# An encoder trunk on one core: order of the first loads, zero products on TensorE, and the place of the sink values' negation

## The chip, the core and the metric

The kernel runs on one NeuronCore of a Trainium2 chip. The metric is the device time of one execution in microseconds (us). The kernel before took 1389.4 us, the median of three runs (1389.08 to 1389.6).

## What is computed

The program is two layers of an encoder over 512 tokens of width 1024, all in float32:

```
for l in range(2):
    h = rms_norm(x, attn_norm_g[l])
    z = h @ w_in[l]                       # q, k, v of two attentions, two gates
    qa, ka, va, qb, kb, vb, ga, gb = split(z)
    qa, ka = rope(rms_norm(qa)), rope(rms_norm(ka))     # cos/sin of positions
    ya = window_gqa(qa, ka, va, sink_a[l]) @ w_proj_a[l]
    yb = neighbourhood_attn(rms_norm(qb), rms_norm(kb), vb, rel_bias_b[l]) @ w_proj_b[l]
    x = x + (sigmoid(ga) * ya + sigmoid(gb) * yb) @ w_out[l]
    h = rms_norm(x, ffn_norm_g[l])
    x = x + (silu(h @ w_gate[l]) * (h @ w_up[l])) @ w_down[l]
```

The sink is one extra logit per head in the softmax of the first attention; the softmax there needs the sink values and their negation.

## The kernel before

**Number format.** Every float32 product is made of three products in a faster format: each factor is split into a high part (a rounding copy, on ScalarE) and a low part (the difference, on VectorE), and high x high, high x low and low x high are added up in PSUM. So an operand costs a copy on ScalarE and a subtraction on VectorE, and each 128x512 tile of a product costs three matmuls.

**Start of the program.** x comes in eight chunks of 128 columns (`x_load`, SyncE's DMA queue, 256 KB each). The first product is q of layer 0: for each chunk k the routine `start` (line 1174) transposes the four 128x128 blocks of the chunk on TensorE, ScalarE writes the high part of the scaled chunk, the copy xT and its square, and VectorE writes the low part and adds up the squares. Then four groups of three matmuls (one per token block b = 0 to 3) use chunk k. `token_matmul` (line 881) calls `start(k + 1)` behind the group of b = 0, so that in TensorE's queue the transposes of chunk k + 1 stand between the group b = 0 of chunk k and its groups b = 1, 2, 3. The engines take their instructions in the order in which they are written; one that waits holds back all behind it on its engine.

**The first weights.** The four slabs of `w_in` that this product needs (two chunks of rows each) are loaded whole and split on the engines (`first_load`, `first_parts`, lines 529 and 541): slab 0 through ScalarE's queue in two transfers, slabs 1 to 3 through GpSimd's. GpSimd's queue also brings the positions, the head norms' gains, the sinks and the rest of the constants (`cst[:, P:]`, line 735, which has the table of rotary frequencies). The identity for the transposes comes first on SyncE's queue (line 709).

**Norm gains.** `attn_norm_g` and `ffn_norm_g` are loaded as 32 rows of 128 (`vec`, line 711, ScalarE's queue, ahead of slab 0), transposed at once, and read as columns of `vecT` by `gain` (line 742). ScalarE needs the first of them for the high part of chunk 0.

**Tables.** `chain_tables` (line 751) prepares what the heads need: it copies the positions into rows 64 to 67 of `vec2`, negates the sinks (`nsnk`, line 754), transposes `vec2` on TensorE (line 758; the head gains and positions turn into columns, `vec2T`), and works out sine and cosine on VectorE and ScalarE (lines 765 to 782) from `vec2T` and `cst`. It is a generator: a planner with a cost model runs the program once without emitting it, and between two groups of matmuls it lets a chain go on when its `Need` is met, by the model's times of the tiles that it names. The order found is then the program's order on every engine. The model keeps one time per tile, that of its last writer in program order. So `Need("pe", [vec2])` looks at the copy of the positions on VectorE, which is the last to write `vec2`; the hardware waits of the transpose go by all writers of `vec2`, transfers among them.

Of the kernel before, what the change touches and what calls it, by code (L numbers as in the profile page):

```python
# [12 lines left out]
F32 = mybir.dt.float32  # L13
# [3 lines left out]
ALU = mybir.AluOpType  # L17
AX = mybir.AxisListType

P = 128  # L20
# [4 lines left out]
NB = S // P  # L25
# [61 lines left out]
def by_columns(ap):  # L87

    return ap.rearrange("p (r cc c) -> p cc r c", r=8, c=8)


def held(ap):
    return ap.rearrange("p (cc r c) -> p cc r c", r=8, c=8)
# [116 lines left out]
def trunk(ctx: ExitStack, tc: tile.TileContext, a: dict, out: bass.AP, lay: Layout):  # L210
    nc = tc.nc
    PS = bass.MemoryType.PSUM
    cp = ctx.enter_context(tc.tile_pool(name="cp", bufs=1))
# [7 lines left out]
    def nm(s):  # L221
        uid[0] += 1
        return f"{s}_{uid[0]}"
# [7 lines left out]
    def buf(shape, dtype=F32):  # L231

        n = int(np.prod(shape))
        x = lay.place(n, dtype)
        t = arenas[dtype][:, x : x + n]
        if len(shape) == 2:
            t = t.rearrange("p (a b) -> p a b", b=shape[1])
        elif len(shape) == 3:
            t = t.rearrange("p (a b c) -> p a b c", b=shape[1], c=shape[2])
        return t  # L240
# [4 lines left out]
    def act(dtype=F32):  # L245
        return buf([S], dtype)

    def mm_bank():
        return pm.tile([P, S], F32, tag="mm", name=nm("mm"))

    def at_bank():
        return pa.tile([P, S], F32, tag="at", name=nm("at"))
# [42 lines left out]
    def touch(aps, start, end):  # L295
        for x in aps:
            o = name_of(x)
            if isinstance(o, int):
                lay.touch(o, steps[0], start, end)
# [36 lines left out]
    T = Engine(nc.tensor, "pe")  # L336
    V = Engine(nc.vector, "dve")
    A = Engine(nc.scalar, "act")
    G = Engine(nc.gpsimd, "pool")
    Q = Engine(nc.sync, "dma")  # L340
    AQ = Engine(nc.scalar, "dma")
# [187 lines left out]
    def first_load(i):  # L529

        n1, n2, ((_, ap),) = plan[i]
        raws[i] = buf([n1, n2])
        ap = ap.rearrange("(k p) n -> p k n", p=P)
        if i:
            GQ.dma_start(raws[i], ap)
        else:
            for k in range(2):
                AQ.dma_start(raws[i][:, k], ap[:, k])
        highs[i], lows[i] = buf([n1, n2], F32R), buf([n1, n2], F32R)

    def first_parts(k):
        raw, h, lo = raws[k // 2][:, k % 2], highs[k // 2][:, k % 2], lows[k // 2][:, k % 2]
        A.copy(h, raw)
        V.tensor_tensor(lo, raw, h.bitcast(F32), ALU.subtract)
# [142 lines left out]
    ident = cst[:, C_ID : C_ID + P]  # L687
    rev = cst[:, C_REV : C_REV + P]
    rev2 = cst[:, C_REV + 64 : C_REV + 64 + P]
    maskA = cst[:, C_MA : C_MA + 3 * P]  # L690
    vec = cp.tile([32, P], F32, tag="vec", name="vec")
    vec2 = cp.tile([P, P], F32, tag="vec2", name="vec2")
    vecT = cp.tile([P, 32], F32, tag="vecT", name="vecT")
    vec2T = cp.tile([P, P], F32, tag="vec2T", name="vec2T")
    ones = cp.tile([P, 2], F32, tag="ones", name="ones")
    magic = cp.tile([P, 32], I32, tag="magic", name="magic")
    G.memset(vec2, 0.0)
    G.memset(ones, 1.0)
    G.memset(magic, 0x5F3759DF)
# [3 lines left out]
    def x_load(c):  # L703
        t = act().rearrange("p (b n) -> p b n", b=NB)
        Q.dma_start(t, xv[:, :, P * c : P * c + P])
        xin.append(t)


    Q.dma_start(ident, a["consts"][:, :P])
    for i, n in enumerate(("attn_norm_g", "ffn_norm_g")):  # L710
        AQ.dma_start(vec[16 * i : 16 * i + 16], a[n].rearrange("l (k p) -> (l k) p", p=P))
    first_load(0)
    for c in range(KD):
        x_load(c)
    posi = cp.tile([P, P], I32, tag="posi", name="posi")
    for h in range(2):
        GQ.dma_start(
# [12 lines left out]
    gqa = cp.tile([P, 2, DEPTH, HD], F32, tag="gqa", name="gqa")  # L730
    for i, n in enumerate(("q_norm_a", "k_norm_a")):
        GQ.dma_start(gqa[:, i], a[n].rearrange("l d -> (l d)").unsqueeze(0).to_broadcast([P, DEPTH * HD]))
    snk = cp.tile([P, DEPTH, 8], F32, tag="snk", name="snk")
    GQ.dma_start(snk, a["sink_a"].rearrange("l h -> (l h)").unsqueeze(0).to_broadcast([P, DEPTH * 8]))
    GQ.dma_start(cst[:, P:], a["consts"][:, P:])
    warm = cp.tile([P, 2], F32, tag="warm", name="warm")
    A.copy(warm, ones)
    ps = at_bank()
    T.transpose(ps[:, :32], vec, ident[:32, :32])
    V.tensor_copy(vecT, ps[:, :32])  # L740

    def gain(norm, k):
        c = 16 * (norm % 2) + 8 * (norm // 2) + k
        return vecT[:, c : c + 1]

    xT = [buf([S]) for _ in range(KD)]
    nsnk = cp.tile([P, DEPTH, 8], F32, tag="nsnk", name="nsnk")
    gb = cp.tile([P, DEPTH], F32, tag="gb", name="gb")
    trig = cp.tile([P, 2, NB, 32], F32, tag="trig", name="trig")

    def chain_tables():
        yield Need("dve", [posi, snk, gqa])
        V.tensor_copy(vec2[64:68], posi[64:68])
        V.tensor_scalar(nsnk, snk, -1.0, None, ALU.mult)
        yield Need("pe", [vec2], [at_slots])
        at_slots.take()
        ps = at_bank()
        T.transpose(ps[:, :P], vec2, ident)
        yield Need("dve", [ps])
        V.tensor_copy(vec2T, ps[:, :P])  # L760
        at_slots.give(clock["dve"])
        posf = vec2T[:, 64:68]
        V.scalar_tensor_tensor(gb, vec2T[:, 0:2], HD ** -0.5, vec2T[:, 2:4], ALU.mult, ALU.mult)
        v3 = lambda t: t[:, : NB * 32].rearrange("p (b f) -> p b f", b=NB)
        ang = v3(act())
        for b in range(NB):
            V.tensor_scalar(ang[:, b, :], cst[:, C_INV : C_INV + 32], posf[:, b : b + 1], None, ALU.mult)
        yield Need()
        for i, shift in enumerate((0.25, 0.0)):
            n, r = v3(act()), v3(act())  # L770
            V.tensor_scalar(n, ang, INV_2PI, shift, ALU.mult, ALU.add)
            V.tensor_scalar(n, n, ROUND_MAGIC, None, ALU.add)
            V.tensor_scalar(n, n, -ROUND_MAGIC, None, ALU.add)
            yield Need()
            V.scalar_tensor_tensor(r, n, -TWO_PI_1, ang, ALU.mult, ALU.add)
            V.scalar_tensor_tensor(r, n, -TWO_PI_2, r, ALU.mult, ALU.add)
            V.scalar_tensor_tensor(r, n, -TWO_PI_3, r, ALU.mult, ALU.add)
            yield Need()
            if shift:
                V.tensor_scalar(r, r, HALF_PI, None, ALU.add)  # L780
            V.tensor_scalar(r, r, PI_LO, -PI_LO, ALU.min, ALU.max)
            A.activation(trig[:, i], r, AF.Sin)
            yield Need()
        done.add("trig")


# [31 lines left out]
    class Norm:  # L818
# [8 lines left out]
        def chunk(self, k):  # L827
            split(xT[k], self.xh[k], self.xl[k], scale=gain(self.i, k))
            sq = act()
            A.activation(sq, xT[k], AF.Square)  # L830
            if self.acc is not None:
                V.tensor_tensor(sq, sq, self.acc, ALU.add)
            self.acc = sq
            if k == KD - 1:
                done.add(f"acc{self.i}")
# [338 lines left out]
    def start(nrm, k):  # L1174

        ps = at_bank()
        for b in range(NB):
            T.transpose(ps[:, P * b : P * b + P], xin[k][:, b, :], ident)
        if k:
            first_parts(k)  # L1180
        A.activation(held(nrm.xh[k]), by_columns(ps), AF.Copy, scale=gain(0, k))
        if not k:
            first_parts(k)
        A.copy(held(xT[k]), by_columns(ps))
        V.scalar_tensor_tensor(nrm.xl[k], xT[k], gain(0, k), nrm.xh[k].bitcast(F32), ALU.mult, ALU.subtract)
        sq = act()
        A.activation(sq, xT[k], AF.Square)
        if nrm.acc is not None:
            V.tensor_tensor(sq, sq, nrm.acc, ALU.add)
        nrm.acc = sq  # L1190
        if k == KD - 1:
            done.add("acc0")

    def layer(l):
# [158 lines left out]
        if l == 0:  # L1353
            spawn(chain_tables())
# [366 lines left out]
```

## Time and profile before

| what | us |
|---|---|
| median of 3 runs | 1389.4 (1389.08 to 1389.6) |
| the profiled execution, its own time | 1389.13 |
| its span, first to last instruction | 1387.4 |
| TensorE busy, share of the span | 1370.7, 99% |
| VectorE busy | 910.7, 66% |
| ScalarE busy | 708.3, 51% |
| first matmul of a product | 6.80 after the start |

The profiled execution's own time is 1.7 us above its span: that is what lies before the first and behind the last instruction. TensorE (PE in the rows) is the engine that sets the time nearly everywhere; what it misses at the start it doesn't make up. In rows of the timeline the first number is the start, the second the duration in us; "out<-in" are the tiles, buffer numbers left out, so `vec` stands for `vec` and `vec2` alike; x4 is a count; brackets hold the idle time of the engine ahead of the row and who ended it. A duration of several merged rows reaches to the end of the last.

### The profile page before, as it was taken

How to read it: one execution, taken by the hardware profiler on the slowest of the kernel's cores; microseconds unless marked ns; L12 is line 12 of the kernel's file. 1: busy time of each engine (PE TensorE's matmuls, PEld its weight loads, DVE VectorE, ACT ScalarE, POOL GpSimd, SP SyncE). 2: the span in 40 equal slices, each digit the busy share in tenths (PEclk: the TensorE clock that was granted, in tenths of full speed). 3: DMA queues.
4: the chain of work that ended last, by engine and by line, in shares of the span. 5: the costliest groups of instructions: out<-in, count | busy, mean ns of one | idle time of the engine just before them, and what ended most of it. 6: DMA issues, size and time to landing. Idle time of an engine off the chain costs nothing.

```text
span 1387.4 us, 20895 instructions
## 1 busy us (share of the span) xinstructions
PE 1370.7 (99%) x8042; PEld 1211.2 (87%) x8042; DVE 910.7 (66%) x1702; ACT 708.3 (51%) x1171; POOL 317.3 (23%) x326
## 2 busy tenths in 40 slices
PE   8999999999999999999999999999999999999998
PEld 6888888888899999999888888888888999999996
DVE  5875878555976657575648667784578757575663
ACT  6476667634643333343545675675356434333441
POOL 4542222310221110111353422223012110111110
PEclk9999999999999999999999999999999999999999
DMA  8998888864766484735899978879457583654645
GB/s 213 183 172 142 158 161 155 173 165 127 151 148 152 106 197 93 182 93 106 160 189 188 166 140 160 155 140 217 142 121 151 123 213 88 156 122 121 146 86 119
DMA packets 197331, 207.45 MB, mean 150 GB/s; under 512 B 25568, under 2 KB 167056, under 8 KB 197232
## 3 DMA queue, kind: packets, MB, share of 16 engines
q0 software_dynamic: 134976, 141.54, 54.6%
q1 hardware_dynamic: 61904, 64.04, 15.9%
q8 instruction: 63, 1.03, 0.3%
q10 hardware_dynamic: 352, 0.54, 0.1%
q14 instruction: 36, 0.29, 0.1%
HBM read 193.51 MB, written 2.10 MB: 141 GB/s over the span
## 4 chain that ended last, share of the span: by engine, by line
PE 90%; DVE 2%; issue 2%; ACT 2%; DMA 2%; POOL 0%; POOLq 0%; ACTq 0%
PE mm L310 71%; PE at L310 19%; ACT arena L310 2%; DVE arena L310 2%; DMA arena<-in_w_down 1%; DMA arena<-in_w_in 1%; DVE sm L310 0%; DMA cst<-in_consts 0%; POOL arena L310 0%; ACT L310 0%; POOL posi L310 0%; POOL vec L310 0%; DVE mm L310 0%; ACT trig L310 0%; ACT sm L310 0%
## 5 line engine op out<-in xcount | busy, mean ns | idle before, releaser
L310 PE MATMUL mm<-arena 128*128 128x512 f32 (+1 forms) x5568 | 1113.1, 355 | 5.8 <-DVE mm L310 3.4
L310 PEld LDWEIGHTS mm<-arena 128*128 128x128 f32 x5568 | 905.0, 190 | 140.7 <-DVE arena L310 4.1
L310 ACT CAST arena<-arena 128x1024 fp32r<-128x1024 f32 (+2 forms) x278 | 235.3, 869 | 213.8 <-DVE arena L310 207.7
L310 DVE TENSOR_TENSOR arena<-arena,arena 128x1024 fp32r<-128x1024 f32 (+2 forms) x268 | 262.1, 993 | 52.1 <-ACT arena L310 51.4
L310 PE MATMUL at<-arena 128*128 128x256 f32 (+1 forms) x1952 | 282.8, 289 | 0.4 <-DVE negm L310 0.4
L310 ACT ACTIVATE arena<-arena 128x1024 fp32r<-128x1024 f32 (+3 forms) x252 | 206.7, 843 | 149.4 <-DMA arena<-in_w_down 77.0
L310 PEld LDWEIGHTS at<-arena 128*128 128x128 f32 x1952 | 259.9, 191 | 13.6 <-DVE negm L310 1.4
L310 DVE TENSOR_TENSOR arena<-arena,mm 128x512 f32<-128x512 f32 x144 | 98.9, 686 | 241.8 <-PE mm L310 240.3
L310 POOL DMA_DIRECT2D arena<-in_w_in x163 | 162.2, 1370 | 303.4 <-ACT arena L310 281.7
L310 POOL DMA_DIRECT2D arena<-in_w_down x96 | 98.1, 1224 | 505.4 <-ACT arena L310 376.7
L310 DVE TENSOR_TENSOR arena<-arena 128x1024 f32<-128x1024 f32 (+4 forms) x196 | 158.0, 823 | 2.4
L310 DVE TENSOR_TENSOR arena<-at,arena 128x512 fp32r<-128x512 f32 (+4 forms) x158 | 104.3, 660 | 30.6 <-ACT arena L310 24.1
L310 ACT CAST arena<-at 128x512 fp32r<-128x512 f32 (+2 forms) x116 | 64.4, 555 | 63.7 <-PE at L310 62.4
L310 PE MATMUL at<-cst,arena 128*128 128x128 f32 x472 | 74.0, 276 | 1.8 <-issue 1.4
L310 ACT ACTIVATE arena<-arena,negm 128x256 f32<-128x256 f32 (+1 forms) x128 | 68.2, 534 | 14.4 <-DVE negm L310 12.4
L310 ACT COPY arena<-at 128x512 f32<-128x512 f32 (+1 forms) x68 | 39.5, 581 | 64.5 <-PE at L310 64.0
L310 PEld LDWEIGHTS at<-cst,arena 128*128 128x128 f32 x472 | 58.1, 141 | 11.9 <-issue 1.8
L310 DVE TENSOR_TENSOR arena<-mm,arena 128x512 f32<-128x512 f32 x72 | 49.1, 686 | 25.3 <-PE mm L310 25.1
L310 DVE CUSTOM_DVE_ANT_0 arena<-at,cst,nsnk 128x256 f32<-128x256 f32 (+1 forms) x64 | 34.4, 547 | 35.0 <-PE at L310 34.4
L310 ACT ACTIVATE arena<-arena,vecT 128x512 fp32r<-128x512 f32 x24 | 17.4, 726 | 54.8 <-DVE arena L310 54.4
L310 DVE CUSTOM_DVE_ANT_0 arena<-at,arena 128x256 f32<-128x256 f32 x64 | 26.3, 420 | 17.3 <-PE at L310 17.0
L310 POOL DMA_DIRECT2D arena<-in_w_up x8 | 8.2, 1030 | 126.7 <-PE mm L310 79.1
(68 smaller groups left out, 423.2 us busy)
## 6 DMA issues: line engine op xcount, KB each, us to landing
arena<-in_w_in POOLq DMA_DIRECT2D x99, 512.0 KB, 7.4
arena<-in_w_down POOLq DMA_DIRECT2D x80, 512.0 KB, 6.7
arena<-in_w_gate SPq DMA_DIRECT2D x20, 1024.0 KB
arena<-in_w_up SPq DMA_DIRECT2D x20, 1024.0 KB
arena<-in_w_in POOLq DMA_DIRECT2D x64, 256.0 KB, 6.4
arena<-in_w_proj_a POOLq DMA_DIRECT2D x16, 512.0 KB, 7.3
arena<-in_w_proj_b POOLq DMA_DIRECT2D x16, 512.0 KB, 7.1
arena<-in_w_out SPq DMA_DIRECT2D x16, 512.0 KB
```

The costliest lines, as they stand in the source:

```text
L310: f(*args, **kw)
```

## The change

- `vec` holds only `attn_norm_g`, 16 rows, and comes on SyncE's queue behind the identity and ahead of x. `ffn_norm_g` goes into rows 32 to 47 of `vec2`, on SyncE's queue behind the eight chunks of x; `gain` reads it from `vec2T`.
- The two transfers of slab 0 are the first on ScalarE's queue.
- The high and low part of slab 0's first rows are written ahead of those of x's chunk 0, as the other chunks have it already.
- Seven float32 products of zeros, 128x128, are put ahead of the first transpose, and three behind the transposes of chunk 0. Their operand is the tile `trig`, cleared by GpSimd as its first act and later overwritten by the cosines.
- The negation of the sinks stands behind the sine and cosine; the first `Need` of the chain names the positions alone.

```diff
+    def turn_over(n):
+        ps = mm_bank()
+        for _ in range(n):
+            T.matmul(ps[:, :P], idle, idle, start=True, stop=True)
+
+    G.memset(idle, 0.0)
     G.memset(vec2, 0.0)
...
+    first_load(0)
     Q.dma_start(ident, a["consts"][:, :P])
-    for i, n in enumerate(("attn_norm_g", "ffn_norm_g")):
-        AQ.dma_start(vec[16 * i : 16 * i + 16], a[n].rearrange("l (k p) -> (l k) p", p=P))
-    first_load(0)
+    Q.dma_start(vec, a["attn_norm_g"].rearrange("l (k p) -> (l k) p", p=P))
     for c in range(KD):
         x_load(c)
+    Q.dma_start(vec2[32:48], a["ffn_norm_g"].rearrange("l (k p) -> (l k) p", p=P))
...
     A.copy(warm, ones)
+    turn_over(7)
     ps = at_bank()
-    T.transpose(ps[:, :32], vec, ident[:32, :32])
+    T.transpose(ps[:, :16], vec, ident[:16, :16])
...
     def gain(norm, k):
-        c = 16 * (norm % 2) + 8 * (norm // 2) + k
-        return vecT[:, c : c + 1]
+        t, c = (vec2T, 32) if norm % 2 else (vecT, 0)
+        c += 8 * (norm // 2) + k
+        return t[:, c : c + 1]
...
     def chain_tables():
-        yield Need("dve", [posi, snk, gqa])
+        yield Need("dve", [posi])
         V.tensor_copy(vec2[64:68], posi[64:68])
-        V.tensor_scalar(nsnk, snk, -1.0, None, ALU.mult)
         yield Need("pe", [vec2], [at_slots])
...
             A.activation(trig[:, i], r, AF.Sin)
             yield Need()
+        yield Need("dve", [snk, gqa])
+        V.tensor_scalar(nsnk, snk, -1.0, None, ALU.mult)
         done.add("trig")
...
-        if k:
-            first_parts(k)
+        if not k:
+            turn_over(3)
+        first_parts(k)
         A.activation(held(nrm.xh[k]), by_columns(ps), AF.Copy, scale=gain(0, k))
-        if not k:
-            first_parts(k)
         A.copy(held(xT[k]), by_columns(ps))
```

Behind the first twenty microseconds the instructions of both programs stand in the same order on every engine, apart from `vec2T` in the place of `vecT` where the FFN's gains are read. Three places of the start show what moves.

SyncE's queue, as a difference, first rows of the program: `vec` is the tile of `attn_norm_g`, `vec_76` is `vec2`, `arena_72` takes x.

```order
 L310 DMA cst<-in_consts 128x128
+L310 DMA vec<-in_attn_norm_g 16x128
 L310 DMA arena_72<-in_x 128x4x128 x8
+L310 DMA vec_76<-in_ffn_norm_g 16x128
 L310 DMA arena_73<-arena_73 64x512 x4
```

The two gains now stand on this queue, one ahead of the eight chunks of x, the other behind them.

TensorE before, from the group b = 0 of chunk 1 to the transposes of chunk 3 (`mm_2` to `mm_5` are the banks of the token blocks 0 to 3, `at_8` and `at_10` the transposes of the chunks 2 and 3, `at_9_181` the transpose of `vec2`; DMAHW and DMASW are counters of transfers, HW of the queues of SyncE and ScalarE, SW of GpSimd's):

```order
L310 MATMUL mm_2_121<-arena1_73 128x512 [waits Activation_49]
L310 MATMUL mm_2_121<-arena1_73 128x512 [waits DVE_49] x2
L310 MATMUL at_8_166<-cst_74,arena0_72 128x128 [waits DMAHW7_49]
L310 MATMUL at_8_166<-cst_74,arena0_72 128x128 x3
L310 MATMUL mm_3_122<-arena1_73 128x512 x3
L310 MATMUL at_9_181<-cst_74,vec2_76 128x128 [waits DMASW5_49,DMASW3_49,DMASW6_49,DMASW2_49,DVE_49]
L310 MATMUL mm_4_123<-arena1_73 128x512 x3
L310 MATMUL mm_5_124<-arena1_73 128x512 x3
L310 MATMUL mm_2_121<-arena1_73 128x512 [waits Activation_49]
L310 MATMUL mm_2_121<-arena1_73 128x512 [waits DVE_49] x2
L310 MATMUL at_10_199<-cst_74,arena0_72 128x128 [waits DMAHW0_49,PE_49]
```

The same piece of TensorE's queue now (`mm_3` to `mm_6` are the banks, `at_10` and `at_12` the transposes of the chunks 2 and 3, `at_11_190` the transpose of `vec2`):

```order
L310 MATMUL mm_3_130<-arena1_73 128x512 [waits Activation_49]
L310 MATMUL mm_3_130<-arena1_73 128x512 [waits DVE_49] x2
L310 MATMUL at_10_178<-cst_74,arena0_72 128x128 [waits DMAHW6_49]
L310 MATMUL at_10_178<-cst_74,arena0_72 128x128 x3
L310 MATMUL at_11_190<-cst_74,vec2_76 128x128 [waits DMASW5_49,DMASW6_49,DMASW3_49,DMAHW4_49,DMASW2_49,DVE_49]
L310 MATMUL mm_4_131<-arena1_73 128x512 x3
L310 MATMUL mm_5_132<-arena1_73 128x512 x3
L310 MATMUL mm_6_133<-arena1_73 128x512 x3
L310 MATMUL mm_3_130<-arena1_73 128x512 [waits Activation_49]
L310 MATMUL mm_3_130<-arena1_73 128x512 [waits DVE_49] x2
L310 MATMUL at_12_211<-cst_74,arena0_72 128x128 [waits DMAHW7_49]
```

The transpose of `vec2` has moved up by one group of three matmuls, and among its waits there is a new one on a counter of the hardware queues, DMAHW4: the transfer of `ffn_norm_g`.

VectorE, as a difference, around the copy of the positions (`vec_76` is `vec2`; the three rows behind `nsnk` are the low parts of slab and x and the sum of squares, for chunk 2):

```order
 L310 TENSOR_TENSOR arena_72<-arena_72 128x512
 L310 CAST vec_76<-posi 4x128
-L310 TENSOR_SCALAR nsnk<-snk 128x16
 L310 TENSOR_TENSOR arena_73<-arena_72,arena_73 128x512
 L310 SCALAR_TENSOR_TENSOR arena_73<-arena_72,vecT,arena_73 128x512
```

The negation no longer stands ahead of chunk 2's parts; it comes back behind the second sine.

More of the change, by code (lines that the diff above doesn't have):

```diff
@@ L690, in trunk @@
     maskA = cst[:, C_MA : C_MA + 3 * P]
-    vec = cp.tile([32, P], F32, tag="vec", name="vec")
+    vec = cp.tile([16, P], F32, tag="vec", name="vec")
     vec2 = cp.tile([P, P], F32, tag="vec2", name="vec2")
-    vecT = cp.tile([P, 32], F32, tag="vecT", name="vecT")
+    vecT = cp.tile([P, 16], F32, tag="vecT", name="vecT")
     vec2T = cp.tile([P, P], F32, tag="vec2T", name="vec2T")
@@ L696, in trunk @@
     magic = cp.tile([P, 32], I32, tag="magic", name="magic")
+    trig = cp.tile([P, 2, NB, 32], F32, tag="trig", name="trig")
+    idle = trig[:, 0].rearrange("p b f -> p (b f)")
+    def turn_over(n):
[3 more added lines that the diff above has]
+    G.memset(idle, 0.0)
     G.memset(vec2, 0.0)
@@ L737, in trunk @@
     A.copy(warm, ones)
+    turn_over(7)
     ps = at_bank()
-    T.transpose(ps[:, :32], vec, ident[:32, :32])
-    V.tensor_copy(vecT, ps[:, :32])
+    T.transpose(ps[:, :16], vec, ident[:16, :16])
+    V.tensor_copy(vecT, ps[:, :16])
     def gain(norm, k):
-        c = 16 * (norm % 2) + 8 * (norm // 2) + k
-        return vecT[:, c : c + 1]
+        t, c = (vec2T, 32) if norm % 2 else (vecT, 0)
+        c += 8 * (norm // 2) + k
+        return t[:, c : c + 1]
     xT = [buf([S]) for _ in range(KD)]
@@ L748, in trunk @@
     gb = cp.tile([P, DEPTH], F32, tag="gb", name="gb")
-    trig = cp.tile([P, 2, NB, 32], F32, tag="trig", name="trig")
     def chain_tables():
-        yield Need("dve", [posi, snk, gqa])
+        yield Need("dve", [posi])
         V.tensor_copy(vec2[64:68], posi[64:68])
-        V.tensor_scalar(nsnk, snk, -1.0, None, ALU.mult)
         yield Need("pe", [vec2], [at_slots])
```

## The prediction

> **What bounds the kernel now.** I read the page first, then the chain of waits, then the timelines of the first 40 us, since every changed line acts there. The page's first rows:
>
> ```profile
> span 1387.4 us, 20895 instructions
> PE 1370.7 (99%) x8042; PEld 1211.2 (87%) x8042; DVE 910.7 (66%) x1702; ACT 708.3 (51%) x1171; POOL 317.3 (23%) x326
> ```
>
> PE is busy for all but 16.7 us. So what PE loses or saves at the start should come out at the end one for one. The chain of waits, taken up to 60 us, says from where:
>
> ```profile
> 3.94 7.82 DMA arena<-in_w_in
> 11.75 0.28 issue
> 12.04 4.75 DMA cst<-in_consts
> ...
> 36.16 1.02 PE at L310 x8
> 37.18 4.23 PE mm L310 x18
> ```
>
> Transfers lead up to about 17 us; from 36 us on the chain is PE behind PE. Now PE alone, in order of time ("mm" matmuls of the product, "at" transposes):
>
> ```profile
> 4.09 0.28 PE L310 MATMUL at<-cst,vec 32*128 32x32 f32 x1 [4.09 <-DMA vec<-in_ffn_norm_g]
> 4.40 1.12 PE L310 MATMUL at<-cst,arena 128*128 128x128 f32 x4
> 6.80 2.18 PE L310 MATMUL mm<-arena 128*128 128x512 f32 x3 [1.28 <-ACT arena L310]
> 8.78 1.05 PE L310 MATMUL at<-cst,arena 128*128 128x128 f32 x4
> 9.48 4.53 PE L310 MATMUL mm<-arena 128*128 128x512 f32 x12
> 13.86 0.60 PE L310 MATMUL at<-cst,arena 128*128 128x128 f32 x4
> 14.21 0.94 PE L310 MATMUL mm<-arena 128*128 128x512 f32 x3
> 14.99 0.27 PE L310 MATMUL at<-cst,vec 128*128 128x128 f32 x1
> 15.02 1.85 PE L310 MATMUL mm<-arena 128*128 128x512 f32 x7
> 17.55 0.50 PE L310 MATMUL mm<-arena 128*128 128x512 f32 x1 [0.68 <-DVE arena L310]
> ...
> 18.55 0.60 PE L310 MATMUL at<-cst,arena 128*128 128x128 f32 x4
> 18.90 3.02 PE L310 MATMUL mm<-arena 128*128 128x512 f32 x12
> 21.76 0.60 PE L310 MATMUL at<-cst,arena 128*128 128x128 f32 x4
> ```
>
> Three losses: PE stands until 4.1; it runs slow up to about 13 (four transposes take 1.1 us, later 0.6); and at 17.5 it waits for VectorE. The slow clock by itself, the matmuls from 10.1 to 12.6 us:
>
> ```profile
> 9.48 3.33 PE L310 MATMUL mm<-arena 128*128 128x512 f32 x7
> ```
>
> Seven slow matmuls take 3.33 us, seven fast ones (15.02) 1.85: 0.21 us more for each. VectorE's wait:
>
> ```profile
> 12.45 0.22 DVE L310 CAST vec<-posi 4x128 f32<-4x128 int32 x1
> 16.72 0.17 DVE L310 TENSOR_SCALAR nsnk<-snk 128x16 f32<-128x16 f32 x1 [4.05 <-DMA snk<-in_sink_a]
> 18.68 0.28 DVE L310 COPY vec2T<-at 128x128 f32<-128x128 f32 x1
> 19.07 0.67 DVE L310 TENSOR_SCALAR arena<-cst,vec2T 128x32 f32<-128x32 f32 x4
> 19.66 0.68 DVE L310 TENSOR_TENSOR arena<-arena,arena 128x512 fp32r<-128x512 f32 x1
> ```
>
> The negation of the sinks holds chunk 2's parts back for 4.05 us. The change takes this wait away.
>
> **The change part by part.** First what it puts ahead. SyncE's and ScalarE's queues:
>
> ```profile
> 1.19 0.44 ACTq L310 DMA_DIRECT2D vec<-in_ffn_norm_g  x1
> 1.20 6.67 SPq L310 DMA_DIRECT2D arena<-in_x  x8
> ...
> 1.66 1.09 ACTq L310 DMA_DIRECT2D arena<-in_w_in  x2
> ```
>
> Slab 0 is issued 0.92 us earlier (1.66 to 0.74); x about 0.44 later, the price of one small issue. The ten products of zeros stand where PE is idle: seven before 4.1, where PE waits for the gains, three behind the first transposes, where it waits 1.28 for ScalarE. No row shows one; between a slow transpose (1.12 / 4 = 0.28) and a slow 512-column matmul (0.48) seven take 2.0 to 3.3 us and three 0.8 to 1.4, so at worst 0.1 shows. They should bring the fast clock some microseconds ahead, worth up to 9 x 0.21 = 1.9 us on the nine matmuls of chunk 0 behind 9.48. Putting slab 0's copy ahead takes one copy of some 0.6 us from PE's wait at 6.80. GpSimd's memset delays its transfers by about 0.2 us. The narrower `vec` and the other place of the FFN gains cost nothing: same instructions, 100s of us before their use. All of this brings PE earlier to the transpose of `vec2`: to about 12 us if all of it works, 14.5 if none does (transposes of chunk 2 now end at 13.86 + 0.60).
>
> Now what PE meets there. The transpose of `vec2` is ahead of three groups of chunk 1 (nine matmuls) and waits for `ffn_norm_g`, which is on SyncE's queue behind all of x. When is that queue done? DMA rows of two stretches, 17 to 17.5 us and 17.5 to 18 (q1 is SyncE's queue; the second stretch has no row of it):
>
> ```profile
> q1 hardware_dynamic: 39, 0.02, 13.0%
> ```
>
> ```profile
> q0 software_dynamic: 137, 0.18, 154.0%
> ```
>
> The last bytes of x move at about 17.4, nearly 10 us after the last issue, because GpSimd's slabs share the engines. x's first chunk was there at 4.4 (PE's transposes), with the other seven already issued or on their way: the queue serves in order of issue. So 8 KB behind x land at about 18.0: last bytes 17.4, and some tenths for its own packets and its signal. The bounds: 17.5 (the start of x's traffic is fuller now) and 18.8 (0.44 later issue, packets of GpSimd's queue in between). No row of this case shows two transfers of one queue in conflict. [...]
>
> So PE stands from 12 to 18.0, and all that was won before is spent there. Behind it: the transpose (0.3), then 9 matmuls of chunk 1 and 3 of chunk 2, ready long since, before the transposes of chunk 3. Twelve take 21.76 - 18.90 = 2.86 now. Chunk 3's transposes start at 18.0 + 0.3 + 2.86 = 21.16, in place of 18.55: **+2.6 us**. VectorE's turn: the copy of `vec2T` comes at about 18.4 (18.68 now), so the tables and chunk 3's low part (19.66) stay where they were and are no longer late for PE. `nsnk` itself, 0.17, hides beside PE.
>
> The clock. What a pause does to it shows at the end of the program: PE's last rows, and the column PEclk (the third number from the end) in three stretches:
>
> ```profile
> 1380.44 0.60 PE L310 MATMUL at<-cst,arena 128*128 128x128 f32 x4
> 1382.46 0.63 PE L310 MATMUL at<-cst,arena 128*128 128x128 f32 x4 [1.42 <-issue]
> ```
>
> ```profile
> 1381.00:1384.00 3.00, 0.67 (x5) 0.42 (x4) 1.28 (x2) 0.59 (x1) 0.00 (x0) 1.00 0.51 159
> 1384.00:1385.00 1.00, 0.00 (x0) 0.00 (x0) 0.00 (x0) 0.00 (x0) 0.00 (x0) 0.96 0.29 93
> 1385.00:1386.00 1.00, 0.00 (x0) 0.00 (x0) 0.00 (x0) 0.00 (x0) 0.00 (x0) 0.50 0.53 169
> ```
>
> The clock halves at 1384.9 (0.96 is 0.08 us at half), 3.9 us after the last dense work and in spite of four transposes in between. A pause of 6 us is longer, so I take it that PE resumes slow. How long? At the start it became fast near 12.7, after work without a gap since about 8.2: 4.5 us. At 0.476 us a matmul these are 9.5 matmuls, times 0.21: **+2.0 us**. Bounds: 0, and 3.0 if it takes as long as from the first matmul (6.80) to 12.7. [...]
>
> From chunk 3's transposes on, both programs have the same order and the same dependences (transposes, ScalarE's copies, VectorE's low part, products), and the chain is PE: I give nothing back and add nothing. Sum, on the profiled execution's own 1389.13: +2.6 +2.0 = +4.6, **1393.7**. The median is 0.27 above that execution, within what three runs scatter.
>
> **Rivals.**
> - *The clock stays fast over the pause*, or PE comes so late (14.5) that the pause is under 3.9 us. Then +2.6 alone: 1391.7. For it: the fall was seen once only. Against: 6 is well over 3.9.
> - *The gains come early* and PE doesn't stop. The point that decides is about 15.5 us: landing + 0.3 + 2.86 = 18.55. Its place is next VectorE's table step, which reads `cst`:
>
> ```profile
> cst<-in_consts POOLq DMA_DIRECT2D x1, 336.0 KB, 6.7
> ```
>
> Issued at 12.04, it is there at 18.7. Chunk 3's low part follows at 18.7 + 0.6, against 19.66 now; PE, done with chunk 2 at some 16.5, waits for it, and chunk 3's products end 0.4 to 0.7 earlier than now: 1388.6. So the wait for the sinks was hiding a wait for the constants. For it: only an overtaking on SyncE's queue. Against: x's first chunk landed first.
> - *All the change is for*: gains early, and `cst` 3 us sooner because slab 0 leaves the queues sooner. Then the 0.6 of the copy, 1.9 of the clock and the 1.6 that PE now stands or runs late between 16.9 and 18.5 are won: 4.1, 1385.0. It needs two transfers to land earlier than any row suggests.
>
> **How the numbers follow.** Forecast (pause and slow clock) 0.78, pause alone 0.12, gains early 0.07, all won 0.03. The range reaches from the second case with a landing at 17.6 (1391.3) to a landing at 18.8 with the longest slow time (1389.13 + 3.4 + 3.0 = 1395.5): 1391.3 to 1395.6. A measurement of this kernel tells about 0.2% (2.8 us) from no change, so "slower" begins at 1392.2. Slower: nearly all of the forecast and a fifth of the second case, 0.80. Same: the rest of the second and the third, 0.17. Faster: 0.03.
>
> **What would show it.** In the new profile: no wait of `nsnk`; the first product before 6.8; at the transpose of `vec2` a pause of 5 to 6 us, ended by `in_ffn_norm_g` near 18; the matmuls behind it at 0.43 to 0.48 each for 4 to 5 us; chunk 3's transposes near 23.2 in place of 18.55; the start of the sums (36.16) later by the same 4.6. Wrong if that pause is missing or ends before 15.5, or if PE's distance shrinks between chunk 3 and 41 us.

## The result, and the profile after

The changed kernel takes 1396.17 us (median of six, 1395.32 to 1398.66), the kernel before 1389.41 (median of six, 1389.08 to 1390.05): a ratio of 1.0051, with a 95% interval of 1.0040 to 1.0061. It is slower by 6.8 us where 4.3 on the median (4.6 on the profiled execution) were forecast, and just outside the range. Its profiled execution took 1396.52, the span in it:

```profile
span 1393.3 us, 20937 instructions
PE 1373.8 (99%) x8062; PEld 1215.1 (87%) x8062; DVE 911.2 (65%) x1702; ACT 708.0 (51%) x1171; POOL 317.5 (23%) x327
```

So the span grew by 5.9 us; the rest of that execution's 7.4 lies outside it (3.2 us now, 1.7 before). TensorE in order of time, the rows that answer to those of before:

```profile
5.68 1.11 PE L310 MATMUL at<-cst,arena 128*128 128x128 f32 x4 [1.11 <-DMA arena<-in_x]
7.73 1.74 PE L310 MATMUL mm<-arena 128*128 128x512 f32 x3
9.31 0.60 PE L310 MATMUL at<-cst,arena 128*128 128x128 f32 x4
9.66 3.01 PE L310 MATMUL mm<-arena 128*128 128x512 f32 x12
12.52 0.60 PE L310 MATMUL at<-cst,arena 128*128 128x128 f32 x4
19.63 0.45 PE L310 MATMUL at<-cst,vec 128*128 128x128 f32 x1 [6.51 <-DMA vec<-in_ffn_norm_g]
19.73 4.44 PE L310 MATMUL mm<-arena 128*128 128x512 f32 x12
24.00 0.60 PE L310 MATMUL at<-cst,arena 128*128 128x128 f32 x4
```

The pause is there, at the transpose of `vec2`, and the FFN's gains end it, at 19.63. The chain of waits runs through the same transfer, from its issue to its landing:

```profile
7.49 12.01 DMA vec<-in_ffn_norm_g
19.50 0.14 issue
19.63 0.45 PE at L310
20.08 4.09 PE mm L310 x12
...
41.61 1.02 PE at L310 x8
```

The clock around the pause (stretches of 1 us; the third number from the end is the granted clock, 1.00 or 0.50, so a mean of 0.60 is 0.8 us at half):

```profile
15.00:16.00 1.00, 0.00 (x0) 0.00 (x0) 0.70 (x2) 0.49 (x1) 0.00 (x0) 0.99 1.08 323
16.00:17.00 1.00, 0.00 (x0) 0.00 (x0) 0.00 (x0) 0.00 (x0) 0.00 (x0) 0.50 1.20 370
22.00:23.00 1.00, 1.00 (x4) 0.81 (x3) 0.00 (x0) 0.00 (x0) 0.00 (x0) 0.60 0.00 0
```

It halves at 15.98 and is back at 22.80, 3.2 us behind the end of the pause. VectorE no longer waits for the sinks:

```profile
37.97 0.17 DVE L310 TENSOR_SCALAR nsnk<-snk 128x16 f32<-128x16 f32 x1
```

The transposes of chunk 3 start 5.45 us later than before (24.00 against 18.55), and the ones-sums too (41.61 against 36.16). By the end 0.45 us more have come on, about half of it at a pause near 390 us (1.89 us long, 1.66 in before).

### The profile page after: what moved, and what is told of

Its sections match the earlier page's. It is cut to its first block, busy times and chain, and to the rows that moved or that the text cites. A ratio compares the mean times of both kernels' runs of the same rounds, so it can differ in the third digit from the quotient of the medians.

```text
span 1393.3 us, 20937 instructions
## 1 busy us (share of the span) xinstructions
PE 1373.8 (99%) x8062; PEld 1215.1 (87%) x8062; DVE 911.2 (65%) x1702; ACT 708.0 (51%) x1171; POOL 317.5 (23%) x327
## 4 chain that ended last, share of the span: by engine, by line
PE 90%; DVE 2%; ACT 2%; issue 2%; DMA 2%; SPq 0%; POOL 0%; DVEq 0%; POOLq 0%; ACTq 0%
PE mm L310 71%; PE at L310 19%; ACT arena L310 2%; DVE arena L310 2%; DMA arena<-in_w_down 1%; DMA vec<-in_ffn_norm_g 1%; SPq L310 0%; DVE sm L310 0%; POOL arena L310 0%; ACT L310 0%; DVE mm L310 0%; ACT trig L310 0%; DVEq L1728 0%; ACT sm L310 0%; DVE den L310 0%
## 5 line engine op out<-in xcount | busy, mean ns | idle before, releaser
L310 ACT ACTIVATE arena<-arena,vec2T 128x512 fp32r<-128x512 f32 x16 | 11.6, 726 | 47.5 <-DVE arena L310 47.5
```

The costliest lines, as they stand in the source:

```text
L310: f(*args, **kw)
```

## The experiments

Thirteen kernels, each beside runs of the kernel before on the same chip. "Ratio" is to before, with its 95% interval; "span" is that of the profiled execution.

| kernel | edit, in words | median, us | ratio | span |
|---|---|---|---|---|
| changed kernel | | 1396.17 | 1.0051 (1.0040 to 1.0061) | 1393.3 |
| e1_gain_early | FFN gains on ScalarE's queue | 1388.84 | 1.0003 (0.9994 to 1.0012) | 1386.3 |
| e2_late_gain_alone | before + late gains | 1394.37 | 1.0035 (1.0023 to 1.0048) | 1393.5 |
| e3_sink_move_alone | before + only the sinks' move | 1388.80 | 0.9997 (0.9988 to 1.0006) | 1387.0 |
| e4_hold_clock | changed + products in the pause | 1394.14 | 1.0031 (1.0020 to 1.0043) | 1390.9 |
| e8_slab_second | changed, slab 0 behind the gains | 1394.10 | 1.0040 (1.0026 to 1.0054) | 1392.2 |
| e10_hold_slabs | changed, next slabs held back | 1398.07 | 1.0059 (1.0047 to 1.0072) | 1396.0 |
| e12_no_zeros | changed without zeros | 1395.42 | 1.0042 (1.0029 to 1.0056) | 1391.5 |
| e5_early_no_zeros | e1 without zeros | 1389.04 | 0.9997 (0.9988 to 1.0006) | 1387.0 |
| e6_early_tables | e1 + constants early | 1389.95 | 1.0003 (0.9994 to 1.0012) | 1387.8 |
| e7_tables_no_zeros | e6 without zeros | 1389.02 | 0.9996 (0.9988 to 1.0005) | 1387.0 |
| e9_low_later | e6, a low part later | 1388.65 | 0.9994 (0.9985 to 1.0003) | 1388.0 |
| e11_tables_hold | e9, next slabs held back | 1390.02 | 1.0000 (0.9991 to 1.0009) | 1389.2 |
| e13_fill_pause | e9 + products in a later pause | 1387.84 | 0.9987 (0.9979 to 0.9996) | 1386.2 |

My theory was the prediction's: the wait for the gains behind x, plus the clock that falls in it. The rivals were that the time goes elsewhere (the zeros, slab 0 in x's way), and that the loss stays when the wait is gone.

### Is it the wait for the gains?

**e1_gain_early**, the changed kernel with one line moved:

```diff
     first_load(0)
+    AQ.dma_start(vec2[32:48], a["ffn_norm_g"].rearrange("l (k p) -> (l k) p", p=P))
...
-    Q.dma_start(vec2[32:48], a["ffn_norm_g"].rearrange("l (k p) -> (l k) p", p=P))
```

Expected: 

> The changed kernel with one line moved: the FFN gains are loaded on ScalarE's queue right behind slab 0, not on SyncE's behind x. All orders on TensorE and VectorE stay. Theory (the transpose of vec2 waits for this transfer, and behind it VectorE's table step waits for the constants, there at 17.9 in the changed kernel's trace): no pause at the transpose, chunk 4's transposes at about 20.3 (27.21 in the changed kernel, 21.76 in the one before), time about 1387.9. Rival 1 (nothing else holds PE): chunk 4's transposes at about 18.9, time about 1386.5. Rival 2 (the pause has another cause): 1396 as before.

TensorE goes through without a pause:

```profile
13.50 0.27 PE L310 MATMUL at<-cst,vec 128*128 128x128 f32 x1
16.39 0.60 PE L310 MATMUL at<-cst,arena 128*128 128x128 f32 x4
```

VectorE meets the next wait, the one that the prediction named:

```profile
17.43 0.68 DVE L310 TENSOR_SCALAR arena<-cst,vec2T 128x32 f32<-128x32 f32 x4 [0.78 <-DMA cst<-in_consts]
```

The whole loss is gone with this one line: 1388.84, which can't be told from before. It is 0.9 above what I expected, though chunk 4's transposes come 0.5 sooner than expected (19.77; 21.76 in before). The ones-sums are 1.27 us earlier than in before (34.89), the profiled span is 1.1 shorter; over eleven executions the median span is 1387.1, against 1387.3.

**e2_late_gain_alone**, the kernel before with only this of the change:

```diff
-    for i, n in enumerate(("attn_norm_g", "ffn_norm_g")):
-        AQ.dma_start(vec[16 * i : 16 * i + 16], a[n].rearrange("l (k p) -> (l k) p", p=P))
+    AQ.dma_start(vec, a["attn_norm_g"].rearrange("l (k p) -> (l k) p", p=P))
...
         x_load(c)
+    Q.dma_start(vec2[32:48], a["ffn_norm_g"].rearrange("l (k p) -> (l k) p", p=P))
...
```

Expected: 

> The kernel before with one part of the change alone: the FFN gains in rows 32 to 47 of vec2, loaded on SyncE's queue behind x. Orders on TensorE and VectorE stay as before, so six matmuls of chunk 1 and three of chunk 2 stand behind the transpose of vec2, not twelve. Theory: the pause begins at 15.0 and ends near 18.0, when x is done in the traffic of the kernel before; chunk 3's transposes at 20.4 in place of 18.55, time about 1391.3, up to 1393 if the clock falls in the pause. Rival (the order of the other loads or the zeros make the loss): 1389.4.

```profile
20.01 0.45 PE L310 MATMUL at<-cst,vec 128*128 128x128 f32 x1 [4.62 <-DMA vec<-in_ffn_norm_g]
20.11 4.19 PE L310 MATMUL mm<-arena 128*128 128x512 f32 x9
```

1394.37, 1.4 us over the most that I expected: the landing was again taken too early, at 18 in place of 20. Most of the loss comes from this one move. It has a side effect: with one issue less ahead of it, slab 0 is issued at 1.19 in place of 1.66, and x's first transposes start at 5.77 in place of 4.40, though x itself is issued no later (1.18).

**e8_slab_second** puts ScalarE's queue back as it was (both gains, then slab 0); `vec2` still has its late rows 32 to 47, the early copy goes to rows whose values nobody uses:

```diff
-    first_load(0)
     Q.dma_start(ident, a["consts"][:, :P])
-    Q.dma_start(vec, a["attn_norm_g"].rearrange("l (k p) -> (l k) p", p=P))
+    AQ.dma_start(vec, a["attn_norm_g"].rearrange("l (k p) -> (l k) p", p=P))
+    AQ.dma_start(vec2[48:64], a["ffn_norm_g"].rearrange("l (k p) -> (l k) p", p=P))
+    first_load(0)
```

Expected: 

> The changed kernel with ScalarE's queue as in the kernel before: the attention gains and one more 8 KB copy of the FFN gains (into unused rows of vec2) ahead of slab 0; the FFN gains that are used stay behind x. Theory (slab 0 ahead of x's first chunk makes x late, 5.6 in place of 4.35 for chunk 0 and 19.3 in place of 17.9 for chunk 7): the pause ends near 18.1 in place of 19.6, time about 1394.8. Rival (x's end is set by GpSimd's transfers alone): the pause ends at 19.6 again, 1396.

```profile
4.50 0.88 PE L310 MATMUL at<-cst,arena 128*128 128x128 f32 x4
...
18.77 0.45 PE L310 MATMUL at<-cst,vec 128*128 128x128 f32 x1 [6.13 <-DMA arena<-in_w_in]
18.87 4.49 PE L310 MATMUL mm<-arena 128*128 128x512 f32 x12
```

The brackets name a slab that came last by the profile; the transpose doesn't read it, so the row gives only the time at which its own waits were over. That is 0.9 earlier than in the changed kernel (the median is 2.1 lower, but the intervals overlap), and x's first chunk is used at 4.50 in place of 5.68. With slab 0 issued at 0.74 or 1.19 the first transposes start at 5.35 to 5.88 (twelve kernels), with it at 1.66 at 4.40 to 4.70 (before, e3, e8). In e8 x is also issued 0.46 earlier than in the changed kernel; e2, where x's issue didn't move, shows that slab 0 alone puts x's first chunk off by over a microsecond. That it puts off x's end too, as I expected here, isn't shown: e12 and e4, with slab 0 at the head, have their pause end at 18.27 and 18.64.

**e10_hold_slabs** asks why the gains land so late. GpSimd's queue is held behind a small copy until TensorE has turned x's fourth chunk, so that the next slabs of `w_in` (keys and values) don't move beside the end of x; the planner is told of it:

```diff
-        plan_pair(w_in, KA0, KD)
+        plan_pair(w_in, KA0, KD, later_h=10.2 if l == 0 else 0.0, later_l=6.0 if l == 0 else 0.0)
...
+        if k == 3 and not lay.dry:
+            nc.gpsimd.tensor_copy(junk, xT[k][:, :2])
```

Expected: 

> The changed kernel with layer 0's key-value slabs held on GpSimd's queue until x's fourth chunk of transposes is there, so that they don't move beside the tail of x. Theory A (the late landing of the FFN gains is x's tail sharing the transfer engines with the key-value slabs): gains land at 17.8 to 18.3, chunk 3's transposes near 22.5 instead of 24.0, 1394 to 1395, unless the key-value slabs' own later landing (near 25 instead of 21.3) gives it back. Theory B (x's own queue scatters by execution, whatever moves beside it): gains land anywhere between 18.3 and 20, 1395 to 1397.

Transfers from 17 to 18 us by queue (q1 is SyncE's, q0 GpSimd's; packets, MB, share of the engines' time), the changed kernel:

```profile
q0 software_dynamic: 339, 0.35, 156.2%
q1 hardware_dynamic: 36, 0.01, 7.9%
```

and e10_hold_slabs:

```profile
q1 hardware_dynamic: 44, 0.02, 6.3%
q0 software_dynamic: 5, 0.01, 1.5%
```

TensorE in e10_hold_slabs:

```profile
18.16 0.45 PE L310 MATMUL at<-cst,vec 128*128 128x128 f32 x1 [4.98 <-DMA vec<-in_ffn_norm_g]
18.26 4.99 PE L310 MATMUL mm<-arena 128*128 128x512 f32 x12
23.09 0.60 PE L310 MATMUL at<-cst,arena 128*128 128x128 f32 x4
```

With GpSimd's queue quiet the gains are there at 18.16, 1.5 us earlier. That agrees with theory A in this execution, but doesn't show it: with the changed kernel's loads, and GpSimd's queue as full (335 and 351 packets from 17 to 18 us), the pause ends at 18.64 in e4 and 18.27 in e12. The end of x's queue moves from one execution to the next. The widest step is between two kernels with the same loads in the same order on every queue: SyncE's last packet is done at 17.36 in before, at 20.69 in e3_sink_move_alone. From 19 to 20 us that queue is empty in before; in e3 it still has these packets:

```profile
q1 hardware_dynamic: 13, 0.01, 3.3%
```

That is theory B's scatter, and more than I had allowed; what moves the end isn't shown. As a remedy the hold fails: 1398.07. The held slabs are issued only at 25.18, and TensorE falls behind: against before by 5.0 us at the first ones-sums, 7.1 at 46 us, and 9.8 from 400 us on.

### Is it the clock?

**e4_hold_clock**, the changed kernel with 24 products of zeros into an unused part of the bank, ahead of the transpose of `vec2`:

```diff
         ps = at_bank()
+        if not lay.dry:
+            for _ in range(24):
+                nc.tensor.matmul(ps[:, P : 2 * P], idle, idle, start=True, stop=True)
         T.transpose(ps[:, :P], vec2, ident)
```

Expected: 

> The changed kernel with 24 more products of zeros right ahead of the transpose of vec2, in the pause (24 at about 0.24 fill 5.8 us). The transfer that ends the pause stays. Theory (the clock falls in the pause, and the twelve matmuls behind it take 4.27 in place of 2.86): they take 2.9, chunk 3's transposes at 22.6 in place of 24.0, time about 1394.7, and runs scatter less. Rival (the clock isn't it): 1396.

```profile
12.13 5.52 PE L771 MATMUL at<-trig 128*128 128x128 f32 x48
18.64 0.30 PE L310 MATMUL at<-cst,vec 128*128 128x128 f32 x1 [0.98 <-DMA vec<-in_ffn_norm_g]
18.70 3.01 PE L310 MATMUL mm<-arena 128*128 128x512 f32 x12
21.54 0.60 PE L310 MATMUL at<-cst,arena 128*128 128x128 f32 x4
```

The wait stays; the twelve matmuls take 2.84 us (18.70 to 21.54) in place of 4.27 (19.73 to 24.00). So the clock is a term of its own, 1.4 us here, and in this run products of zeros held it up. In this execution the gains were also there 1.0 earlier. The median is 2.0 lower, though the ends of the two intervals still overlap.

### What do the zeros and the sinks bring?

**e3_sink_move_alone**, the kernel before with only the negation moved:

```diff
-        yield Need("dve", [posi, snk, gqa])
+        yield Need("dve", [posi])
         V.tensor_copy(vec2[64:68], posi[64:68])
-        V.tensor_scalar(nsnk, snk, -1.0, None, ALU.mult)
...
+        yield Need("dve", [snk, gqa])
+        V.tensor_scalar(nsnk, snk, -1.0, None, ALU.mult)
         done.add("trig")
```

Expected: 

> The kernel before with the negation of the sinks moved behind the sines, nothing else. Theory (the wait for the sinks hides one for the constants, there at 18.8): VectorE's idle time moves from nsnk to the step that reads cst, nearly as long less the work done in between; chunk 3's transposes about 17.3 but chunk 4's at about 21.2 in place of 21.76; time about 1388.8. Rival (nothing takes its place): PE's wait of 1.2 near 17.5 goes and stays gone, 1388.1 or less.

```profile
18.64 0.68 DVE L310 TENSOR_SCALAR arena<-cst,vec2T 128x32 f32<-128x32 f32 x4 [1.11 <-DMA cst<-in_consts]
```

The wait for the sinks was hiding that for the constants: 4.05 us of one go, 1.11 of the other come up, and the median moves by 0.3 us, which can't be told from nothing.

**e12_no_zeros** and **e5_early_no_zeros**, the changed kernel and e1_gain_early without the ten products:

```diff
-    turn_over(7)
...
-        if not k:
-            turn_over(3)
```

Expected of the first: 

> The changed kernel without its ten products of zeros, all else kept. Theory (what the change costs is the wait for the FFN gains and the clock that it loses; the zeros only bring TensorE to that wait sooner, so that the pause is longer): first matmuls slow as before, TensorE at the wait near 14 in place of 13.1, a pause of 4.5 to 6 us, chunk 3's transposes where the landing puts them (23 to 24.3), 1393.5 to 1396. If the zeros cost something of their own (the time outside the span was 1.7 to 3.2 us with them and 1.7 to 1.8 without in the pairs run so far): own time minus span 1.7 to 1.8 in every execution, and a median 0.3 to 1.5 below the changed kernel's 1396.17, about 1395.

Expected of the second: 

> The kernel with the FFN gains early (e1) and without the ten products of zeros. Theory (the constants hold VectorE, so an earlier clock is spent in that wait): within 0.5 us of e1. Rival (the earlier clock is worth its nine matmuls of 0.21): 1.9 us slower than e1.

```profile
18.27 0.44 PE L310 MATMUL at<-cst,vec 128*128 128x128 f32 x1 [4.52 <-DMA vec<-in_ffn_norm_g]
```

The zeros do warm the clock (12 matmuls at 9.66 take 3.01 with them; 4.54 in e5 at 9.97), but both pairs end within what can be told apart: 1396.17 and 1395.42, 1388.84 and 1389.04. Whether they cost time outside the span stays open. Without zeros that time is 1.7 to 1.8 us in 42 of 43 executions (e2, e3, e5, e7, e12; one of e12 has 2.1). With them 27 of 77 have 2.0 to 3.2, but none of e4's six and of e13's eleven. So it goes with the zeros, yet they don't always bring it.

### Where does a gain at the start go?

**e6_early_tables** brings the frequencies early too; **e7_tables_no_zeros** is the same without the zeros:

```diff
+    AQ.dma_start(vec2[32:48], a["ffn_norm_g"].rearrange("l (k p) -> (l k) p", p=P))
+    AQ.dma_start(cst[:, C_INV:], a["consts"][:, C_INV:])
...
-    Q.dma_start(vec2[32:48], a["ffn_norm_g"].rearrange("l (k p) -> (l k) p", p=P))
...
-    GQ.dma_start(cst[:, P:], a["consts"][:, P:])
+    GQ.dma_start(cst[:, P:C_INV], a["consts"][:, P:C_INV])
```

Expected of e6: 

> The kernel with the FFN gains early (e1), and the 32 columns of rotary frequencies of the constants as well on ScalarE's queue behind them, apart from the rest of cst. Theory (the constants are what holds VectorE in e1): no wait at the table step, chunk 4's transposes at about 19.1, time about 1386.8, 1 us less than e1. Rival (VectorE or PE is held by something else): as e1.

Expected of e7: 

> As e6, without the ten products of zeros. Theory (with no transfer to wait for, the clock of the first 13 us counts): 1 to 1.9 us slower than e6. Rival (the head is bound elsewhere): as e6.

ScalarE, then TensorE in e6_early_tables:

```profile
20.93 1.06 ACT L310 ACTIVATE arena<-arena 128x1024 fp32r<-128x1024 f32 x1 [3.34 <-DMA arena<-in_w_in]
```

```profile
23.13 0.73 PE L310 MATMUL mm<-arena 128*128 128x512 f32 x2 [2.12 <-ACT arena L310]
...
25.08 4.58 PE L310 MATMUL mm<-arena 128*128 128x512 f32 x12
```

A third wait takes the place of the second: ScalarE stands at a part of the key slab, whose transfer is not in, and chunk 4's high part is queued behind. The clock falls too, from 25.17 to 28.59: twelve matmuls take 4.42 us (25.08 to 29.50). The rival held. e7, which I expected slower by 1 to 1.9, has a median 0.9 lower (the intervals overlap): there TensorE comes to this place later, ScalarE waits for the slab for only 0.35, and the clock stays up.

**e9_low_later** moves that part behind, **e11_tables_hold** also holds the slabs as in e10:

```diff
-        plan_pair(w_in, KA0, KD)
+        plan_pair(w_in, KA0, KD, later_l=6.0 if l == 0 else 0.0)
```

Expected of e9: 

> As the run with the FFN gains and the rear part of the constant table both on ScalarE's queue behind slab 0 (1389.95 us; chunk 4's transposes at 18.33 us, then matmuls of chunk 5 behind a pause of 2.12 us, since ScalarE stood 3.34 us at the cast of the low part of the key-value slab, whose load lands at 20.91, and the next high part was queued behind that cast). Here the low part's cast stands later in ScalarE's queue. Theory (each wait of the first 25 us is taken over by the next in line, and a pause of over 3 us costs the clock on top): ScalarE goes on to the next high part at once, no pause over 1 us on TensorE before 25 us, no stretch of half clock after 16 us, ones-sums about 33.5 to 34.5, 1386.5 to 1388. Rival (a further wait takes over, here the landing of the second key-value slab at about 21.3): a pause at chunk 5 or 6 again, 1388.5 to 1390.

Expected of e11: 

> Gains and rear part of the constant table on ScalarE's queue behind slab 0, and layer 0's key-value slabs held on GpSimd's queue until x's fourth chunk of transposes is there, their casts later in ScalarE's queue. Theory: no wait on constants or gains, ScalarE not held by the low part, x's last landing not behind 19: chunk 4's transposes near 18, ones-sums 33.5 to 34.5, 1386 to 1388. Rival (a held slab is late at the products of keys and values, whose matmuls follow the chunks): the pause turns up there, 1388.5 to 1391.

In both, TensorE then runs up to the ones-sums without a wait over 0.4 us, and these stand at 33.43 and 33.62, 2.7 and 2.5 us earlier than in before. Yet the profiled spans, 1388.0 and 1389.2, are longer than before's 1387.4. By 46 us e9 has lost 1.5 of its lead and e11 2.2, e9 most of it at a slab (waits of TensorE from 40 to 360 us):

```profile
PE mm L310 <- DMA arena<-in_w_in: 1.2, 1, 1.2
```

The rest, and more, goes near 1067 us in e9 (1.5 us) and near 385 us in e11 (3.3 us). There, at the start of each layer's feed-forward part, TensorE waits for VectorE; in before the second such wait is 1.72 us long, and the 84 matmuls behind it take 11.64:

```profile
1066.88 11.64 PE L310 MATMUL mm<-arena 128*128 128x256 f32 x84 [1.72 <-DVE mm L310]
```

In e9 (row of the timeline, then the clock):

```profile
1065.54 13.15 PE L310 MATMUL mm<-arena 128*128 128x256 f32 x84 [1.85 <-DVE mm L310]
```

```profile
1066.00:1067.00 1.00, 1.00 (x10) 1.00 (x9) 1.00 (x1) 0.36 (x1) 0.00 (x0) 0.85 0.18 38
...
1070.00:1071.00 1.00, 1.00 (x10) 1.00 (x9) 0.69 (x1) 0.11 (x1) 0.98 (x2) 0.94 0.12 5
```

With a wait longer by 0.13 comes a stretch of 3.4 us at half clock (1066.70 to 1070.12), 1.5 us of time. In e11 the first of these waits lasts 3.54, and the 84 matmuls behind it take as long, with a late transfer ahead of it in the chain of waits: ScalarE's row there, then that of TensorE.

```profile
381.57 0.63 ACT L310 ACTIVATE arena<-arena 128x512 fp32r<-128x512 f32 x1 [3.69 <-DMA arena<-in_w_down]
```

```profile
387.91 13.10 PE L310 MATMUL mm<-arena 128*128 128x256 f32 x84 [3.54 <-DVE mm L310]
```

One execution misleads here: e9's profiled one is the second longest of its eleven. Their median span is 1386.0, 1.4 us under that of the runs of before beside it (1387.4); the median time is only 0.5 lower, since 2.1 us lie outside the span in the median (1.8 in before). So by the medians about half of the 2.7 comes through to the end of the span, and more than half of that is lost again outside it. e11's median span is 1388.1.

**e13_fill_pause** puts ten products of the identity into that wait, in e9:

```diff
                 ps[bank] = at_bank()
+            if m == 7 and quads[l, q, w].first and not lay.dry:
+                spare = at_bank()
+                for _ in range(10):
+                    T.matmul(spare[:, :P], ident, ident, start=True, stop=True)
             o = ps[bank]
```

Expected: 

> The kernel in which neither the FFN gains, nor the constants, nor the low part of the key-value slab is waited for (1388.65 us median; executions between 1385.3 and 1388.4 in span), with ten products of the identity with itself in TensorE's pause of 1.7 to 3.5 us near the start of each layer's feed-forward part (384 and 1064 us). They take 0.8 to 1.5 us of the pause and reach no output. Theory (the gain of the start is lost again in part because that pause costs a stretch of 3.4 us at half clock, 1.5 to 1.7 us of time, in some executions): the clock stays fast there in every execution, spans 1385 to 1386.5, their scatter under 1.5 us, median 1387.2 to 1388. Rival (the loss is in late landings, or in time outside the span): scatter and median as without them, 1388.2 to 1389.

```profile
1063.59 2.39 PE L310 MATMUL at<-cst 128*128 128x128 f32 x20
1065.74 11.65 PE L310 MATMUL mm<-arena 128*128 128x256 f32 x84
```

The 84 matmuls take 11.65 again. In the eleven executions of e13 the mean granted clock is never under 0.999 and the spans lie between 1385.3 and 1387.0; in those of e9 it goes down to 0.997, and the spans lie between 1385.3 and 1388.4. The fill is a little too long (2.15 us for a wait of 1.85). The median span is no shorter than e9's (1386.1 against 1386.0): what is gone are a few long executions, three of e9 above 1387.0 and none of e13, and these are few (the two kernels also ran on different chips). At 1387.84 us this is the one kernel that beats both: 0.9987 of before (0.9979 to 0.9996), 0.6% under the changed kernel. Its 0.8 under e9's median lies outside the span, where all eleven have 1.7 to 1.8; that the fill did this isn't shown, and the two intervals overlap.

## Why the prediction was wrong

**The mechanism was right.** The wait for the sinks is gone; TensorE stops at the transpose of `vec2`; the gains behind x (issued at 7.49, landed at 19.50) end the pause; the clock falls in it and the matmuls behind run slow; the loss of the first 24 us comes out at the end. e1 takes it away by moving one transfer, e2 makes most of it by that transfer, e4 takes the clock's part away. The wait that the sinks were hiding came up in e1 and e3, at `cst`, where it was named. The price of the rival with early gains, 1388.6, is close to what e1 took (1388.84), in part by luck: the constants were there at 17.41, not 18.7, and of the 2.0 us that e1 was ahead at chunk 4 it had 1.27 left at the ones-sums.

**The step that failed is the landing of the gains, "at about 18.0", with 18.8 as the later bound.** The transpose started at 19.63: +1.63 us. I had read the end of x's queue from one execution of before (last bytes at 17.4) and carried it over. The "some tenths" behind it were right: from SyncE's last packet to the transpose 0.63 us went by. What was wrong is the end of the queue itself, 19.00. From 18 to 19 us, when in before SyncE's queue was already empty, it still has packets among GpSimd's:

```profile
q0 software_dynamic: 348, 0.35, 175.7%
q1 hardware_dynamic: 14, 0.01, 3.4%
```

The last 50 packets of SyncE's queue (36 and 14) take two microseconds among 687 of GpSimd's (339 and 348). But e4 and e12 ended earlier beside as many, and with the loads of before the queue was done at 17.36 in one trace and at 20.69 in another (e3). Over six kernels that load the gains behind x the queue ended at 17.42 to 19.37 and the transpose started at 18.16 to 20.01. So one execution gave no bound for the end of this queue; why it ended 1.6 us later here stays open.

**The slow clock was put at +2.0 and cost 1.4** (12 matmuls 4.27 in place of 2.86). Behind the end of the pause it lasted 3.2 us here, 4.4 in e10, where the gains landed near the forecast 18.0. There chunk 3's transposes started at 23.09, against the 23.2 of the prediction. So the term was right for its landing (the twelve take 4.83 there, 2.0 over 2.86), and a pause that is 1.5 longer paid less for the clock. One working around it was wrong: from 6.80 to 12.7 us the bound is 2.6, not 3.0, which takes the range to 1395.1. The clock fell 2.9 us into the pause (13.12 to 15.98), where the end of the program had shown 3.9.

**The head of the change came out worse than told.** "The first product before 6.8" was 7.73: x's first chunk was used 1.28 us later (5.68 against 4.40), because slab 0 moves ahead of it (e2: 1.37 later with x issued as before), and I had priced only the 0.44 of the issue. Nothing was lost by it, since TensorE still reached the pause 6.5 us early.

The sum for the profiled execution: 4.6 forecast, +1.63 for the landing, -0.79 for the clock and the transpose (4.37 from its start to chunk 3's, in place of 5.16), +0.45 behind the ones-sums, which I had put at nothing, makes 5.9, its growth in span. Another 1.5 us of that execution lie outside its span; in the other five that part is 1.8 to 3.0. This is not explained. I had taken it for a constant 1.7.

## What to carry to other kernels

Before an operation is given a new source, ask on which queue that source comes and what is ahead of it there; here the 8 KB of gains behind x landed with the tail of the queue (at 19.50, the last packet at 19.00), and that tail moved by a microsecond or more between executions, by up to 3.3 with the same loads. When a wait is removed, look for the wait that it was hiding, and expect that a stretch in which transfers set the pace gives little back until all of them are moved. On TensorE price every pause also by the clock: in these traces one of 1.7 us was free and one of 1.85 cost another 1.5. And before a trace is taken for the kernel, compare its span with the spans of the other executions.

## What the runs showed of the hardware

**In these traces the clock fell behind windows of 3.41 us in which TensorE stood for more than half of the time.** Stretches of half clock that ended within the program lasted 3.4 or 6.8 us: 15.98 to 22.80 in the changed kernel, 1066.70 to 1070.12 in e9. In e10 two falls are seen, at 15.74 and 394.62:

```profile
15.00:16.00 1.00, 0.00 (x0) 0.00 (x0) 0.77 (x2) 0.55 (x2) 0.00 (x0) 0.87 0.78 257
...
394.00:395.00 1.00, 0.44 (x2) 0.47 (x3) 1.00 (x3) 1.00 (x2) 0.00 (x0) 0.81 0.16 38
```

They are 378.88 us apart. Half of the changed kernel's 6.82 us is 3.41, and 378.88 is 111 such steps of 3.413; the full clock in the changed kernel, from 22.80 to 1391.55, is 401 of them (1368.75 / 401 = 3.413). With this step, counted from an edge seen in the same execution, I laid each pause over windows; the traces show the edges, the windows between them are reckoned. Share of the window in which TensorE stood, and what the clock did in the next:

```
kernel    pause              window             idle   next window
before    1065.16-1066.88    1064.07-1067.48    0.50   full
e5        1064.80-1066.53    1064.58-1067.99    0.51   full
changed   1071.09-1072.77    1070.70-1074.12    0.49   full
e9        1063.69-1065.54    1063.29-1066.70    0.54   half
e6          21.01-23.13        21.76-25.17      0.56   half
e10        391.84-394.56      391.21-394.62     0.80   half
e11        384.37-387.91      384.41-387.82     1.00   half
```

For e9: 1.85 / 3.41 = 0.54; in e6 a second pause, 23.86 to 24.39, lies in the window too. In these seven the clock stayed full behind 0.49 to 0.51 and was at half behind 0.54 to 1.00. By this reckoning a wait of 1.7 us is 0.50 of a window: in before 1.72 us cost nothing of the clock, in e9 a wait 0.13 longer cost 1.5 us of time. That may be why executions of one kernel differ by 1.5 to 3 us in span; for those without a trace it is an inference from their mean clock.

**Behind 0.44 idle it did not come back.** In e2 the half clock lasted from 18.49 to 25.32, though by the same reckoning TensorE stood for only 0.44 of the window from 18.49 to 21.91. With 0.20 idle, in e12 (window 17.60 to 21.01), it rose; what the clock does between these isn't shown. That products of zeros count as work for the clock I had supposed, and nothing before these runs showed it; in e4, behind 24 of them, the twelve matmuls took 2.84 us in place of 4.27.
